# One key block of a query pair: split 256-column product against two 128-column products accumulated in PSUM

## The chip, the cores and the metric

One core of a Trainium2 chip runs the whole layer as a single program. The metric is the device time of one execution in microseconds; the median of several runs is compared.

## What is computed

The layer is a hybrid decoder layer: one input projection feeds eight stick-breaking attention heads, a short gated convolution, four memory cross-attention heads and a gate; the branch outputs are normalised by group, gated, projected back and added to the input. The change concerns only the stick-breaking attention (1024 tokens, 8 heads of 64):

```python
z = jnp.einsum('bqhd,bkhd->bhqk', q_blk, k, preferred_element_type=jnp.float32) * scale
before = key_pos[None, :] < q_pos[:, None]
log_not = jnp.where(before, jax.nn.log_sigmoid(-z), 0.0)
suffix = lax.cumsum(log_not, axis=3, reverse=True) - log_not
w = jnp.where(before, jnp.exp(jax.nn.log_sigmoid(z) + suffix), 0.0)
out = jnp.einsum('bhqk,bkhd->bqhd', w.astype(v.dtype), v)
```

All of it is float32.

## The kernel before

The sequence is held in reversed order, so the keys that a query may see lie at and behind its own position, and the stick-breaking products become forward scans along the keys. Float32 products run as several float32r products: each operand is split into hi (the value rounded to float32r) and lo (the exact rest).

Before the attention, the values of all heads are projected while the input arrives (`vh`, laid out as [key, head, hi and lo of 64 columns]). Then an attention part of 12 units runs: six stick-breaking heads, four memory heads, two stick-breaking heads. Each stick-breaking head (`sb_unit`) has four stages `sp` = 0 to 3. A stage takes a pair of query blocks of 128 tokens, blocks 2·sp and 2·sp + 1, against all key blocks from 2·sp on. `sb_scores` makes the scores (line 389, TensorE), the sigmoids (lines 396 and 397, ScalarE), the scan (lines 399 and 401, VectorE) and the weights (line 404, VectorE or GpSimd), for one query block at a time into an SBUF tile `sg`. `sb_apply_steps` then goes through the key blocks in groups `g` of two:

- `tr_step` transposes the weights' 128x128 blocks through TensorE (line 335) into one PSUM tile `tr`, in the order: second key block for both query blocks, first key block for both query blocks. In group 0 the first key block is the first query block's own: the second query block doesn't see it, and only three blocks are transposed.
- `transposed` then makes the hi `wth` by a ScalarE copy (line 341) and the lo `wtl` by a VectorE subtraction (line 342). Of a group's third and last block alone, the lo is written by a second subtraction (line 344) not into `wtl` but into `wth`, right behind the hi.
- `av_step` multiplies by the values: for each key block one product with the hi and one with the lo, 256 columns each (two query blocks), added up in the PSUM tile `av`, columns 0 to 255 (line 429). In group 0 the first key block is treated apart: one product of 256 columns, hi and lo of the one query block side by side (line 426), goes to columns 256 to 511 (`own`).

When the last group is done, `put_y` adds the upper and lower half of `av` (products with the hi and the lo of the values) into `y` by a ScalarE copy (line 351) and a VectorE addition (line 352). Then `put_own_key` does the same with `own` into a small tile (lines 358 and 359), and GpSimd adds its hi part and its lo part to the first query block's columns of `y` (line 361, twice). The small tile `avt` has one buffer; `av` has two, one PSUM bank each.

Between these steps the function `run` lays background work in proportion (`RATIO`, one number per unit): the other input projections (`proj`, line 273, the largest part of all products), the gates, the convolution and the memory's keys and values. Their input weights are split by lines 142 to 145. The instructions of each engine are put in order at build time by the framework's scheduler with a modelled timeline; each engine then works its list off in order, waiting on semaphores. `behind_attention` adds order-only dependencies that keep the projections from running ahead of the attention's transposes and scores.

After the attention come the output projection, the residual and the last norm (lines 760 to 819), which the change leaves alone.

Of the kernel before, what the change touches and what calls it, by code (L numbers as in the profile page):

```python
"""Hybrid decoder layer: stick-breaking attention, short gated convolution and memory
cross-attention heads side by side, group norms, SiLU gate, output projection.

The sequence is processed in reversed order (row j holds token T-1-j), so that the keys of a
query lie after it and the stick-breaking products are forward scans along the free axis:
  state[m] = max(state[m-1] * sigmoid(-z[m-1]), M[m]),   w[m] = sigmoid(z[m]) * state[m],
where M is one at the first key of the row and zero elsewhere.

Float32 products run as float32r passes: each operand is hi + lo, hi = the value rounded to
float32r, lo = the exact rest, and hi*hi + hi*lo + lo*hi carries float32's accuracy.  # L10
"""
# [15 lines left out]
P = 128  # L27
T = 1024
# [15 lines left out]
WARM = 8  # L44
# s, v, p: the engine (scalar, vector, pool) that rounds each weight tile, that takes each
# head's last product of the scan, and that splits its keys
WENG = 'vssssvvvsvvssvvsvvvssvvvvsss'
# [6 lines left out]
def hymba_kernel(ctx, tc, xT, xr, wp, wv, memT, memr, wmem, cols, eye, wout, gfin, out):  # L54
# [18 lines left out]
    def nm(s):  # L73
        uid[0] += 1
        return f"{s}_{uid[0]}"
# [20 lines left out]
    def f(ap):  # L96
        return ap.bitcast(F32)

# [1 line left out]
    col = const.tile([P, 32], F32, name="col")  # L100
# [46 lines left out]

# [1 line left out]
    def row_stats(j):  # L149
# [8 lines left out]

    # the tensor engine's clock comes up on work: zeros, while the first rows load
    for _ in range(WARM):  # L160
# [62 lines left out]

# [1 line left out]
    queue = []  # L225
# [16 lines left out]
    def behind_attention(ins):  # L242
        # order alone: keeps this work from running out ahead of the attention's steps
        if len(marks) > SLACK:
            tc.add_manual_dep(ins.ins, marks[-1 - SLACK].ins.name,
                              mybir.DependencyInfo(mybir.DependencyClass.NoSync, mybir.DependencyReason.DATA),
                              reason="pace")
# [3 lines left out]
    def proj_last(evac, need):  # L251
        # the input's tiles are done with one after the other: the output's weights take them
        wh, wl = next_w()
        ps = [z_tile(), z_tile()]
        for k in range(KC):
            for n, hf in enumerate(HALVES):
                for a, (ww, xx) in enumerate(((wh, xh), (wh, xl), (wl, xh))):
                    ins = nc.tensor.matmul(ps[n], lhsT=ww[:, k, :], rhs=xx[k][:, hf],
                                           start=(k == 0 and a == 0), stop=(k == KC - 1 and a == 2))
                    if a == 0:  # L260
                        behind_attention(ins)
            yield 1.3
        yield from after(need)
        for n, hf in enumerate(HALVES):
            evac(ps[n], hf)
# [65 lines left out]
    def transposed(blocks):  # L331
        # 4 [query, key] blocks: hi and lo of them; of a third and last one, lo comes after hi
        tr = tr_tile()
# [5 lines left out]
        n = len(blocks) * P  # L339
        m = n if n == H else 2 * P  # L340
        nc.scalar.copy(wh[:, 0:n], tr[:, 0:n])  # L341
        nc.vector.tensor_tensor(wl[:, 0:m], tr[:, 0:m], f(wh[:, 0:m]), op=ALU.subtract)  # L342
        if m < n:
            nc.vector.tensor_tensor(wh[:, n:], tr[:, m:n], f(wh[:, m:n]), op=ALU.subtract)
        return wh, wl
# [7 lines left out]

    def put_own_key(y, av, a, t0):
        # one block of queries times their own keys: w's hi, then its lo
        own, oth = (slice(0, 64), slice(64, 128)) if a == 0 else (slice(64, 128), slice(0, 64))
        tmp = small.tile([P, 256], F32, tag="avt", name=nm("avt"), bufs=1)
        nc.scalar.copy(tmp[own], av[oth])
        nc.vector.tensor_tensor(tmp[own], av[own], tmp[own], op=ALU.add)  # L359
        for c in (tmp[own, 0:P], tmp[own, P:]):  # L360
            nc.gpsimd.tensor_tensor(y[own, t0 : t0 + P], y[own, t0 : t0 + P], c, op=ALU.add)  # L361

    def interleave(first, second):
        # steps of two lists of (cost, function), in proportion
        ta, tb = sum(c for c, _ in first), sum(c for c, _ in second)
# [43 lines left out]
    def sb_apply_steps(st, sp, p, a):  # L409
# [9 lines left out]
        def av_step(g):  # L419
            if g == 0:  # L420
                st["av"] = av_tile(True)
            wh, wl = st.pop(("w", g))
            key = lambda j: vh[p][(2 * sp + 2 * g + j) // 4][:, (2 * sp + 2 * g + j) % 4, a, :]
            own, av = st["av"][:, 256:], st["av"][:, 0:256]
            if g == 0:
                nc.tensor.matmul(own, lhsT=key(0), rhs=wh[:, 256:], start=True, stop=True)
            for j, c in ((1, slice(0, 256)), (0, slice(256, H)))[: 2 if g else 1]:
                for n, w in enumerate((wh, wl)):
                    nc.tensor.matmul(av, lhsT=key(j), rhs=w[:, c], start=(g == 0 and n == 0),  # L429
                                     stop=(g == ng - 1 and j == (g == 0) and n == 1))  # L430
            if g == ng - 1:
                put_y(ys[p], av, a, 256 * sp)
                put_own_key(ys[p], own, a, 256 * sp)

# [19 lines left out]
    def stats_sum(st, g, first):  # L454
        # sums over the partitions, as a row, which a DMA lays out as [token, block]
        part = small.tile([P, TB], F32, tag="part", name=nm("part"), bufs=2)
# [13 lines left out]
    def group_stats(c):  # L470
        # the sums of squares of two tiles of 128 columns, a while later
        st = {}
# [99 lines left out]

# [1 line left out]
    def qk_proj(kinds, res):  # L574
# [119 lines left out]
    def attention(units):  # L694
        # steps of all heads in a row: the scores of a stage run one stage ahead of their use
        flat = []
# [15 lines left out]
    def run(steps, bg, ratio):  # L712
        # attention steps, with the other work in proportion
        debt = 0.0
# [44 lines left out]

# [1 line left out]
    post = ctx.enter_context(tc.tile_pool(name="post", bufs=2))  # L761
# [17 lines left out]
    for j in range(TB):  # L779
# [4 lines left out]
        for c in order:  # L784
# [4 lines left out]
                  (0, (0, 1, 2, 3), [tr_tile(), tr_tile()])]  # L789
        # the last rows end on half a bank: less is left to do after the last product  # L790
        todo = [(g, H * hf, H * hf + H) for g in range(3) for hf in range(2)]
# [77 lines left out]
```

## Time and profile before

| what | value |
| --- | --- |
| median of 3 runs | 613.98 us (613.79 to 614.02) |
| the profiled execution, from its first to its last instruction | 614.2 us |
| mean granted TensorE clock | 0.972 of full speed |
| matmuls / weight loads | 2744 / 2744 |
| VectorE, ScalarE, GpSimd instructions counted | 744, 775, 381 |

The profile is that of one execution; what lies around its span isn't recorded, and the span is 0.2 us above the runs' median. In the rows, PE is TensorE's matmuls, PEld its weight loads, DVE VectorE, ACT ScalarE, POOL GpSimd. A row of a group gives line, engine, operation, output and inputs by the program's names, shapes and count, then busy time in us and the mean of one in ns, then the idle time of the engine right before them and what ended it. A row of the timeline gives start and duration in us. A row of stretches gives its bounds and length, the busy time of the engines, the granted clock, the share of DMA and the GB/s.

### The profile page before, as it was taken

How to read it: one execution, taken by the hardware profiler on the slowest of the kernel's cores; microseconds unless marked ns; L12 is line 12 of the kernel's file. 1: busy time of each engine (PE TensorE's matmuls, PEld its weight loads, DVE VectorE, ACT ScalarE, POOL GpSimd, SP SyncE). 2: the span in 40 equal slices, each digit the busy share in tenths (PEclk: the TensorE clock that was granted, in tenths of full speed). 3: DMA queues.
4: the chain of work that ended last, by engine and by line, in shares of the span. 5: the costliest groups of instructions: out<-in, count | busy, mean ns of one | idle time of the engine just before them, and what ended most of it. 6: DMA issues, size and time to landing. Idle time of an engine off the chain costs nothing.

```text
span 614.2 us, 8410 instructions
## 1 busy us (share of the span) xinstructions
PE 565.8 (92%) x2744; PEld 461.6 (75%) x2744; DVE 454.3 (74%) x744; ACT 350.9 (57%) x775; POOL 338.7 (55%) x381
## 2 busy tenths in 40 slices
PE   9999989979899899877979999899988999899995
PEld 5888878758678688755768888778667886688884
DVE  3425159989999996579966766998779668977664
ACT  5646556536685777765745988563645554443232
POOL 2551787454247448987858657448789668411001
PEclk9999999979999999898979999899999999999998
DMA  8931520211302021121313212111011163131311
GB/s 283 403 107 36 137 67 16 57 36 35 104 34 67 5 68 35 34 56 70 98 53 104 70 35 69 34 36 35 4 32 35 35 240 103 69 138 68 114 59 69
DMA packets 22188, 48.36 MB, mean 79 GB/s; under 512 B 7808, under 2 KB 8320, under 8 KB 22144
## 3 DMA queue, kind: packets, MB, share of 16 engines
q1 hardware_dynamic: 22144, 47.82, 24.3%
q8 instruction: 22, 0.36, 0.2%
q14 instruction: 22, 0.18, 0.1%
HBM read 36.78 MB, written 4.20 MB: 67 GB/s over the span
## 4 chain that ended last, share of the span: by engine, by line
DVE 17%; PE 16%; ACT 7%; issue 7%; POOL 6%; DMA 2%; POOLq 0%; DVEq 0%; ACTq 0%
PE tr L802 6%; PE pj L273 3%; PE pj L802 3%; PE z L802 2%; DVE wtl L342 2%; ACT e L546 2%; DVE F L401 2%; DVE F L399 2%; POOL wlo L145 2%; DMA wor<-in_wout 1%; DVE whi L144 1%; POOL sg L404 1%; DVE wol L774 1%; DVE mx L542 1%; DVE y L352 1%
## 5 line engine op out<-in xcount | busy, mean ns | idle before, releaser
L273 PE MATMUL pj<-xh,whi 128*128 128x512 f32 x368 | 150.1, 408 | 4.1 <-DVE mv L681 3.4
L273 PE MATMUL pj<-xl,whi 128*128 128x512 f32 x368 | 146.5, 398 | 0.0
L273 PE MATMUL pj<-xh,wlo 128*128 128x512 f32 x368 | 146.1, 397 | 0.0
L145 POOL TENSOR_TENSOR wlo<-wraw,whi 128x512 fp32r<-128x512 f32 x56 | 81.5, 1469 | 16.2 <-ACT whi L142 11.0
L399 DVE TENSOR_TENSOR_SCAN F<-F,mask 128x513 f32<-128x513 f32 (+2 forms) x64 | 78.8, 1231 | 13.7 <-ACT F L396 11.0
L273 PEld LDWEIGHTS pj<-xh,whi 128*128 128x128 f32 x368 | 70.8, 192 | 17.2 <-DVE mv L681 3.6
L273 PEld LDWEIGHTS pj<-xh,wlo 128*128 128x128 f32 x368 | 70.5, 192 | 14.3
L273 PEld LDWEIGHTS pj<-xl,whi 128*128 128x128 f32 x368 | 70.7, 192 | 12.2
L396 ACT ACTIVATE F<-z,nrq 128x512 f32<-128x512 f32 (+3 forms) x96 | 55.8, 583 | 22.8 <-PE z L389 11.0
L404 POOL TENSOR_TENSOR sg<-sg,F 128x512 f32<-128x512 f32 (+3 forms) x48 | 56.0, 1171 | 20.1 <-DVE F L401 10.3
L342 DVE TENSOR_TENSOR wtl<-tr,wth 128x512 fp32r<-128x512 f32 (+1 forms) x96 | 56.1, 592 | 11.0 <-ACT wth L341 10.1
L361 POOL TENSOR_TENSOR y<-y,avt 64x128 f32<-64x128 f32 x64 | 47.5, 743 | 22.8 <-DVE avt L359 20.1
L341 ACT CAST wth<-tr 128x512 fp32r<-128x512 f32 (+1 forms) x96 | 51.1, 553 | 14.3 <-PE tr L335 12.7
L397 ACT ACTIVATE sg<-z,rq 128x512 f32<-128x512 f32 (+2 forms) x96 | 55.4, 580 | 3.0 <-PE tr L335 2.8
L335 PE MATMUL tr<-ident,sg 128*128 128x128 f32 x288 | 48.4, 285 | 5.6 <-DVE stg L462 2.0
L401 DVE TENSOR_TENSOR_SCAN F<-F,F,mask 128x512 f32<-128x512 f32 (+1 forms) x32 | 43.9, 1371 | 7.6 <-ACT F L396 7.0
L395 POOL MEMSET F<- 128x1 f32 x96 | 8.9, 97 | 72.0 <-DVE F L401 35.8
L814 POOL TENSOR_TENSOR ssf<-ssf,nhalf 128x1 f32<-128x1 f32 x8 | 7.4, 924 | 71.4 <-DVE ssf L811 62.1
L316 POOL TENSOR_TENSOR qs<-qk,q 64x512 fp32r<-64x512 f32 x24 | 32.9, 1377 | 23.9 <-ACT q L315 23.2
L335 PEld LDWEIGHTS tr<-ident,sg 128*128 128x128 f32 x288 | 35.7, 147 | 10.6 <-DVE sg L404 3.1
L429 PE MATMUL av<-wtl,vh 128*128 128x256 f32 x128 | 35.5, 295 | 7.6 <-DVE wtl L342 7.4
L389 PE MATMUL z<-k,q 128*128 128x512 f32 (+2 forms) x96 | 36.2, 377 | 3.1 <-ACT sg L397 2.9
(188 smaller groups left out, 1283.2 us busy)
## 6 DMA issues: line engine op xcount, KB each, us to landing
wraw<-in_wp SPq DMA_DIRECT2D x24, 512.0 KB, 3.3
xs<-in_xr SPq DMA_DIRECT2D x8, 512.0 KB, 8.6
wor<-in_wout SPq DMA_DIRECT2D x8, 512.0 KB, 5.3
acc<-in_xr SPq DMA_DIRECT2D x8, 512.0 KB, 3.4
out<-acc SPq DMA_DIRECT2D x16, 256.0 KB, 2.1
xs<-in_xT SPq DMA_DIRECT2D x7, 512.0 KB, 8.0
qs<-q SPq DMA_DIRECT2D x12, 256.0 KB, 2.9
q<-qs SPq DMA_DIRECT2D x12, 256.0 KB, 2.9
```

The costliest lines, as they stand in the source:

```text
L145: nc.gpsimd.tensor_tensor(lo[:, c], raw[:, c], f(hi[:, c]), op=ALU.subtract)
L273: ins = nc.tensor.matmul(ps, lhsT=ww[:, k, :], rhs=xx[k][:, hf], start=(k == 0 and a == 0), stop=(k == KC - 1 and a == 2))
L335: ins = nc.tensor.transpose(tr[:, i * P : (i + 1) * P], blk, ident)
L341: nc.scalar.copy(wh[:, 0:n], tr[:, 0:n])
L342: nc.vector.tensor_tensor(wl[:, 0:m], tr[:, 0:m], f(wh[:, 0:m]), op=ALU.subtract)
L361: nc.gpsimd.tensor_tensor(y[own, t0 : t0 + P], y[own, t0 : t0 + P], c, op=ALU.add)
L396: nc.scalar.activation(F[:, 1:m], zz[:, 0 : m - 1], AF.Sigmoid, scale=nrq[:, i : i + 1])
L397: nc.scalar.activation(sg[:, c0:c1], zz, AF.Sigmoid, scale=rq[:, i : i + 1])
L399: nc.vector.tensor_tensor_scan(F[:, 0:m], F[:, 0:m], M[:, 0:m], 0.0, ALU.mult, ALU.max)
L401: nc.vector.tensor_tensor_scan(F[:, 0:m], F[:, 0:m], M[:, 130 : 130 + m], prev[:, H - lo : H - lo + 1], ALU.mult, ALU.max)
L404: eng.tensor_tensor(sg[:, c0:c1], sg[:, c0:c1], F[:, 0:w], op=ALU.mult)
L802: nc.tensor.matmul(ps[:, pc], lhsT=yy[:, c, :], rhs=ww[c][:, c0:c1], start=(c == cs[0] and a == 0), stop=(c == cs[-1] and a == 2))
```

## The change

The first key block of group 0 is no longer treated apart. Its hi lies in `wth` and its lo in `wtl` like that of every other block (one subtraction of 384 columns in place of 256 and 128), and it is multiplied by two products of 128 columns, hi and lo, that accumulate in the first 128 columns of `av`. Line 426's product, `put_own_key` and the second half of `av` go; key block 1 comes first and starts the accumulation.

```diff
 def transposed(blocks):
     ...
     n = len(blocks) * P
-    m = n if n == H else 2 * P
     nc.scalar.copy(wh[:, 0:n], tr[:, 0:n])
-    nc.vector.tensor_tensor(wl[:, 0:m], tr[:, 0:m], f(wh[:, 0:m]), op=ALU.subtract)
-    if m < n:
-        nc.vector.tensor_tensor(wh[:, n:], tr[:, m:n], f(wh[:, m:n]), op=ALU.subtract)
+    nc.vector.tensor_tensor(wl[:, 0:n], tr[:, 0:n], f(wh[:, 0:n]), op=ALU.subtract)
     return wh, wl
 ...
-def put_own_key(y, av, a, t0):
-    own, oth = (slice(0, 64), slice(64, 128)) if a == 0 else (slice(64, 128), slice(0, 64))
-    tmp = small.tile([P, 256], F32, tag="avt", name=nm("avt"), bufs=1)
-    nc.scalar.copy(tmp[own], av[oth])
-    nc.vector.tensor_tensor(tmp[own], av[own], tmp[own], op=ALU.add)
-    for c in (tmp[own, 0:P], tmp[own, P:]):
-        nc.gpsimd.tensor_tensor(y[own, t0 : t0 + P], y[own, t0 : t0 + P], c, op=ALU.add)
 ...
     def av_step(g):
         if g == 0:
-            st["av"] = av_tile(True)
+            st["av"] = av_tile()
         wh, wl = st.pop(("w", g))
         key = lambda j: vh[p][(2 * sp + 2 * g + j) // 4][:, (2 * sp + 2 * g + j) % 4, a, :]
-        own, av = st["av"][:, 256:], st["av"][:, 0:256]
-        if g == 0:
-            nc.tensor.matmul(own, lhsT=key(0), rhs=wh[:, 256:], start=True, stop=True)
-        for j, c in ((1, slice(0, 256)), (0, slice(256, H)))[: 2 if g else 1]:
+        av = st["av"]
+        for j, c in ((1, slice(0, 256)), (0, slice(256, H if g else 256 + P))):
             for n, w in enumerate((wh, wl)):
-                nc.tensor.matmul(av, lhsT=key(j), rhs=w[:, c], start=(g == 0 and n == 0),
-                                 stop=(g == ng - 1 and j == (g == 0) and n == 1))
+                nc.tensor.matmul(av[:, 0 : c.stop - c.start], lhsT=key(j), rhs=w[:, c],
+                                 start=(g == 0 and j == 1 and n == 0),
+                                 stop=(g == ng - 1 and j == 0 and n == 1))
         if g == ng - 1:
             put_y(ys[p], av, a, 256 * sp)
-            put_own_key(ys[p], own, a, 256 * sp)
```

The remaining lines of the diff only blank out comments.

## The prediction

> **What bounds the kernel now.** I read the page's busy table first, then the stretches, then single starts in the timeline.
>
> ```profile
> span 614.2 us, 8410 instructions
> PE 565.8 (92%) x2744; PEld 461.6 (75%) x2744; DVE 454.3 (74%) x744; ACT 350.9 (57%) x775; POOL 338.7 (55%) x381
> ```
>
> TensorE is busy for most of the span, but ends of matmuls are modelled there, so the share says only that it comes first. The attention lies between about 85 and 505 us. In the table by stretch (length, then busy time and count of PE, PEld, DVE, ACT, POOL, then the granted clock) its three parts are the first stick-breaking heads, the memory heads, and the last two stick-breaking heads:
>
> ```profile
> 85.00:310.00 225.00, 197.03 (x1032) 164.29 (x1030) 197.72 (x282) 144.59 (x302) 141.40 (x192) 0.95 0.18 51
> 310.00:395.00 85.00, 82.53 (x416) 68.65 (x417) 60.03 (x121) 60.28 (x140) 53.54 (x53) 0.96 0.24 64
> 395.00:505.00 110.00, 102.80 (x510) 83.19 (x509) 88.00 (x131) 57.09 (x124) 76.49 (x82) 0.98 0.17 58
> ```
>
> From 85 to 310 us TensorE and VectorE are both busy for 197 of 225 us: they hold each other up in turn. After that TensorE alone is near full. So work added to TensorE counts wherever it doesn't fall into one of its waits, and work taken from VectorE counts only where TensorE waits for it.
>
> What one product really costs TensorE is the distance from its start to the next start, not its row's duration. The timeline has all the widths close together:
>
> ```profile
> 171.62 0.33 PE L389 MATMUL z<-k,q 128*128 128x384 f32 x1
> 171.79 0.34 PE L389 MATMUL z<-k,qs 128*128 128x384 f32 x1
> ...
> 174.03 0.39 PE L273 MATMUL pj<-xl,whi 128*128 128x512 f32 x1
> 174.26 0.39 PE L273 MATMUL pj<-xh,wlo 128*128 128x512 f32 x1
> 174.48 0.28 PE L389 MATMUL z<-k,q 128*128 128x256 f32 x1
> 174.60 0.28 PE L389 MATMUL z<-k,qs 128*128 128x256 f32 x1
> 174.72 0.60 PE L335 MATMUL tr<-ident,sg 128*128 128x128 f32 x4
> 175.07 0.48 PE L273 MATMUL pj<-xh,whi 128*128 128x512 f32 x1
> 175.40 0.40 PE L273 MATMUL pj<-xl,whi 128*128 128x512 f32 x1
> ```
>
> 512 columns take 0.23 us (174.03 to 174.26), 384 take 0.17 (171.62 to 171.79), 256 take 0.12 (174.48 to 174.60): a straight line of 0.45 ns a column. The four 128-column transposes and the 512-column product behind them take 175.40 − 174.72 = 0.68 us, so a transpose costs (0.68 − 0.23)/4 = 0.11 us, twice what that line gives for 128 columns (0.06).
>
> **The change, part by part.** It touches a place that occurs 32 times: 8 heads by 4 pairs of query blocks, the first pair of key blocks of each (g = 0).
>
> ```profile
> L426 PE MATMUL av<-wth,vh 128*128 128x256 f32 x32 | 10.9, 340 | 12.9 <-DVE wth L344 10.8 <-ACT sg L397 1.2 <-ACT avt L351 0.9
> L429 PEld LDWEIGHTS av<-wth,vh 128*128 128x128 f32 x128 | 24.5, 192 | 3.1 <-ACT wth L341 0.2 <-issue 0.2 <-ACT avt L358 0.2
> L342 DVE TENSOR_TENSOR wtl<-tr,wth 128x512 fp32r<-128x512 f32 x64 | 43.2, 682 | 8.7 <-ACT wth L341 8.2
> L342 DVE TENSOR_TENSOR wtl<-tr,wth 128x256 fp32r<-128x256 f32 x32 | 13.2, 413 | 2.2 <-ACT wth L341 1.9
> L344 DVE TENSOR_TENSOR wth<-tr,wth 128x128 fp32r<-128x128 f32 x32 | 8.9, 279 | 0.0
> L359 DVE TENSOR_TENSOR avt<-av,avt 64x256 f32<-64x256 f32 x32 | 13.3, 414 | 3.3 <-ACT avt L358 2.9
> L358 ACT COPY avt<-av 64x256 f32<-64x256 f32 x32 | 11.7, 366 | 20.6 <-DVE y L352 20.2
> L361 POOL TENSOR_TENSOR y<-y,avt 64x128 f32<-64x128 f32 x64 | 47.5, 743 | 22.8 <-DVE avt L359 20.1
> ```
>
> *TensorE.* One 256-column product (line 426, hi and lo side by side) goes, two 128-column products with the same key come: 768 columns before and after, one matmul and one weight load more. The weight load is hidden: 192 ns rows run beside products that start every 0.12 us. The price of a 128-column float32r product is the open number, since no row has one. Below, the straight line gives 0.06 us: then nothing is added. The nearest row by width, the transpose, gives 0.11: 2 × 0.11 − 0.12 = +0.10 a place. Above, it should not cost more than the 512-column product, 0.23: +0.34 a place, 10.9 us over 32. I take 0.23. This is a choice, not a reading: the transpose already stands at twice the line, so the line doesn't hold at 128 columns, and a transpose, which passes one operand through unchanged, is to me a floor for a product of that width; 0.23 is the only row above it that bounds one.
>
> The Trainium skill, "FP8 and Floating Point Precision", section TensorE Precision Notes, states that true float32 takes four passes through the array. If a narrow float32r product fell back to that, 4 × 128 columns would cost what the 512 row costs, and the total would be the 617.4 worked out below; with one pass it would be 606.5. No row before the change can tell which.
>
> *The wait at line 426.* The own-key product needs the lo that line 344 writes, behind line 342's first subtraction. The first and the last place of those that wait:
>
> ```profile
> 90.83 0.28 DVE L344 TENSOR_TENSOR wth<-tr,wth 128x128 fp32r<-128x128 f32 x1
> 91.26 0.36 PE L426 MATMUL av<-wth,vh 128*128 128x256 f32 x1 [1.06 <-DVE wth L344]
> ...
> 475.99 0.28 DVE L344 TENSOR_TENSOR wth<-tr,wth 128x128 fp32r<-128x128 f32 x1
> 476.42 0.36 PE L426 MATMUL av<-wth,vh 128*128 128x256 f32 x1 [1.46 <-DVE wth L344]
> ```
>
> In 14 of the 32 places, these two the outermost, line 426 starts within 0.15 us of line 344's end; in the other 18 the lo has long been there. Afterwards the first product (key 1, hi) needs only ScalarE's copy, so it slips into the wait (0.12 us), and the wait moves to the second product, which needs one subtraction of 384 columns. That lies between the 256 and 512 rows, (0.413 + 0.682)/2 = 0.55 us, against 0.413 + 0.279 = 0.69: the lo is ready 0.15 us sooner. Queued behind it on TensorE's in-order stream are that place's last three products, then transposes and scores. So a waiting place costs 0.34 − 0.12 − 0.15 = +0.07 us, an unhindered one +0.34: 14 × 0.07 + 18 × 0.34 = **+7.1 us**.
>
> *VectorE.* Line 359 goes (0.414) and the split subtraction saves 0.15: 0.56 us a place, 18 us of 454. It counts where VectorE is what TensorE waits for. At most that is all 14 waiting places, 7.8 us; at least nothing. I take half, **−3.9 us**: line 359 comes after the last product of its pair, and what the next wait needs may be held by a scan or a copy instead.
>
> *ScalarE and GpSimd.* The copies at line 358 (11.7 us) and the adds at line 361 (47.5 us) go. Nothing of TensorE's reads y soon; the waits they end are these:
>
> ```profile
> PE av L426 <- DVE wth L344: 10.8, 10, 2.1
> ACT avt L351 <- POOL y L361: 15.3, 9, 4.2
> ACT avt L358 <- DVE y L352: 20.2, 17, 3.8
> ```
>
> The second and third (engine, what it waited for, us in total, times, longest) hold ScalarE, which is idle 43% of the span; I count them as nothing of their own. If that cover is gone, they are worth up to what ScalarE then delivers late, and that is inside the 7.8 us above. The PSUM tile is free one copy and one add sooner; with two such tiles nobody is shown waiting for it. No DMA and no queue entry of SyncE moves.
>
> **Sum.** 614.2 + 7.1 − 3.9 = 617.4 us on the profiled execution's span; that span is 0.2 above the median of the runs, 613.98, so 617.2 for the median. The three runs lie within 0.04%; I take 0.2%, 1.2 us, as what can be told from no change.
>
> **The rivals.**
>
> *Narrow products are cheap (faster).* At 0.11 us: 18 × 0.10 + 14 × (0.10 − 0.27) − 3.9 = −4.5, 609.7 us; at 0.06: 14 × (−0.27) − 3.9 = −7.7, 606.5. For it speaks the nearest row by width, against it that this row is no product. It decides as soon as the price is under about 0.18 us: 32 × (2 × 0.18 − 0.12) = 7.7 is what the 14 places (14 × 0.27 = 3.8) and the relief (3.9) give back.
>
> *Narrow products are dear, but GpSimd's adds were in VectorE's way (faster).* A scan beside a GpSimd multiply takes far longer than its kind does in the mean:
>
> ```profile
> 91.66 1.29 POOL L404 TENSOR_TENSOR sg<-sg,F 128x512 f32<-128x512 f32 x1
> 91.73 1.77 DVE L401 TENSOR_TENSOR_SCAN F<-F,F,mask 128x256 f32<-128x256 f32 x1
> ...
> L399 DVE TENSOR_TENSOR_SCAN F<-F,mask 128x256 f32<-128x256 f32 x8 | 6.7, 832 | 0.1
> ```
>
> 1.77 against 0.83 us for 256 columns. If a quarter of the removed 47.5 us had stood in VectorE's way, that is 11.9 us, of which 14/32 counts: 5.2; with the whole of VectorE's 7.8 the sum is 614.2 + 7.1 − 13.0 = 608.3. It decides when the relief passes 7.1 us, 0.22 a place. Against it: the adds are of 64 partitions by 128 columns, mostly short, and they come when a pair is finished.
>
> The Trainium skill, "SBUF — State Buffer", section Who interferes with whom, has a VectorE instruction with two SBUF inputs shut out while a GpSimd instruction reads SBUF; the slow scan agrees. By that rule all 47.5 us could block, which would double this rival's gain.
>
> *The terms cancel (no change).* With the whole 7.8 us of relief and no more, the sum is 613.5.
>
> *The order shifts (slower still).* Instructions are put in order by a modelled timeline, which the changed products shift. What an unlucky order costs shows in two neighbouring stretches:
>
> ```profile
> 120.00:140.00 20.00, 15.77 (x73) 12.93 (x73) 17.04 (x26) 8.61 (x19) 8.20 (x14) 0.83 0.08 27
> 140.00:160.00 20.00, 19.91 (x109) 16.79 (x108) 19.17 (x30) 12.29 (x25) 7.10 (x10) 1.00 0.36 105
> ```
>
> TensorE loses 4.2 us in the first and 0.1 in the second, and the clock falls to 0.83 beside the loss. One more such stretch gives 617.4 + 4.1 = 621.5; with no relief either, 614.2 + 10.9 = 625.
>
> **How the numbers follow.** Dear products with half the relief (617.4): 0.50. A worse order on top (621 to 625): 0.10. Cancelling: 0.15. GpSimd's relief: 0.10. Cheap products: 0.15. So faster 0.25, same 0.15, slower 0.60. The range 607 to 625 reaches from nearly the cheap end, 606.5, to no relief at all, 625; for the likeliest case alone it is 613.5 to 625, slower than no change nearly throughout.
>
> **What would show it.** Right: 64 products of 128 columns in the attention at about 0.23 us from start to start where they don't wait; the wait for line 344 gone and a shorter one for line 342 in the same 10 to 14 places; VectorE down by some 18 us and GpSimd by some 47; TensorE's busy time up by 7 to 11. Wrong: starts 0.06 to 0.12 us apart behind the narrow products; scans markedly shorter on VectorE; or the same stage taking another order with other waits.

## The result: 22 us faster, and the profile after

The changed kernel takes 591.57 us (median of 4 runs, 590.72 to 592.65), the kernel before 613.88 beside it: ratio 0.9644, interval 0.9609 to 0.9680. The forecast was 617.2, range 607 to 625.

Page of the changed kernel, its span and busy times:

```profile
span 590.1 us, 8309 instructions
...
PE 556.6 (94%) x2776; PEld 460.2 (78%) x2776; DVE 426.6 (72%) x680; ACT 340.0 (58%) x743; POOL 300.5 (51%) x317
```

VectorE has 27.7 us less (18 were forecast; for the other 9.8 its remaining instructions got shorter), GpSimd 38.2 less (the additions were 47.5; what is left on it lasts longer), and TensorE, with 32 products more, is busy 9 us *less*. The table by stretch shows where:

```profile
85.00:310.00 225.00, 208.76 (x1148) 176.90 (x1147) 193.33 (x264) 147.31 (x307) 129.32 (x162) 0.98 0.20 58
310.00:395.00 85.00, 81.13 (x413) 67.66 (x412) 66.80 (x118) 61.46 (x138) 46.70 (x46) 0.98 0.20 54
395.00:505.00 110.00, 104.54 (x514) 85.55 (x514) 79.68 (x113) 53.87 (x115) 75.37 (x67) 0.99 0.23 76
```

From 85 to 310 us TensorE gets through 1148 products where it got through 1032; 24 of the 116 more are the added ones. The gain is TensorE waiting less, and a granted clock of 0.98 in place of 0.95, not less work for it.

The changed place itself, by groups (the last number is idle time ahead and what ended it):

```profile
L341 DVE TENSOR_TENSOR wtl<-tr,wth 128x384 fp32r<-128x384 f32 x32 | 17.5, 547 | 5.1 <-ACT wth L340 4.8
...
L416 PE MATMUL av<-wtl,vh 128*128 128x128 f32 x32 | 8.9, 279 | 0.0
L416 PE MATMUL av<-wth,vh 128*128 128x128 f32 x32 | 7.2, 226 | 0.0
```

and one such place in the timeline (start, duration):

```profile
185.55 0.28 PE L416 MATMUL av<-wtl,vh 128*128 128x256 f32 x1
185.67 0.22 PE L416 MATMUL av<-wth,vh 128*128 128x128 f32 x1
185.73 0.28 PE L416 MATMUL av<-wtl,vh 128*128 128x128 f32 x1
185.85 0.51 PE L335 MATMUL tr<-ident,sg 128*128 128x128 f32 x3
```

with the weight loads of the same stretch:

```profile
185.55 0.19 PEld L416 LDWEIGHTS av<-wth,vh 128*128 128x128 f32 x1
185.68 0.19 PEld L416 LDWEIGHTS av<-wtl,vh 128*128 128x128 f32 x1
185.81 0.31 PEld L335 LDWEIGHTS tr<-ident,sg 128*128 128x128 f32 x3
```

The first narrow product gives way after 0.06 us, in 30 of the 32 places (in the other two, at half the granted clock, after 0.11). The second gives way after 0.11 to 0.12 in 31 of 32, whatever follows it. Its successor's load starts 0.13 us after its own, and I read it so that the load sets the pace: in the kernel before, no two loads of line 429's products start less than 0.108 us apart at full clock. That is some 0.17 for both narrow products, where the removed product took 0.12: +0.05 us a place, 1.6 us in all, where +0.34 at an unhindered place was forecast. The narrow products never wait (idle 0.0); the wait for VectorE's one subtraction now comes at the 256-column product with the lo. From the list of waits (us in total, times, longest), of the changed kernel:

```profile
PE av L416 <- DVE wtl L341: 13.5, 10, 3.8
```

and of the kernel before, where this stands beside line 426's 10.8:

```profile
PE av L429 <- DVE wtl L342: 7.4, 5, 3.7
```

Together 18.2 us in 15 waits became 13.5 in 10.

### The profile page after: what moved, and what is told of

It is laid out like the page before. It is cut to its first block, busy times and chain, and to the rows that moved or that the text cites. A ratio compares the mean times of both kernels' runs of the same rounds, so it can differ in the third digit from the quotient of the medians.

```text
span 590.1 us, 8309 instructions
## 1 busy us (share of the span) xinstructions
PE 556.6 (94%) x2776; PEld 460.2 (78%) x2776; DVE 426.6 (72%) x680; ACT 340.0 (58%) x743; POOL 300.5 (51%) x317
## 4 chain that ended last, share of the span: by engine, by line
PE 32%; DVE 12%; issue 5%; ACT 3%; POOL 2%; DMA 2%; SPq 1%; POOLq 0%; DVEq 0%; ACTq 0%
PE pj L273 11%; PE tr L789 7%; PE pj L789 4%; PE z L789 3%; DVE wtl L341 2%; DVE F L389 2%; PE z L258 2%; DVE F L387 2%; PE tr L335 2%; PE av L416 1%; DMA part<-stg 1%; POOL sg L392 1%; PE z L527 1%; DVE whi L144 1%; DVE sg L392 1%
## 5 line engine op out<-in xcount | busy, mean ns | idle before, releaser
L273 PE MATMUL pj<-xh,whi 128*128 128x512 f32 x368 | 147.2, 400 | 1.0 <-DVE mv L668 1.0
L273 PEld LDWEIGHTS pj<-xh,whi 128*128 128x128 f32 x368 | 69.4, 189 | 12.7 <-DVE mv L668 1.2
L392 POOL TENSOR_TENSOR sg<-sg,F 128x512 f32<-128x512 f32 (+3 forms) x48 | 62.2, 1298 | 27.6 <-DVE F L389 10.5
L341 DVE TENSOR_TENSOR wtl<-tr,wth 128x512 fp32r<-128x512 f32 (+1 forms) x96 | 59.7, 637 | 9.9 <-ACT wth L340 9.1
L416 PE MATMUL av<-wtl,vh 128*128 128x256 f32 (+1 forms) x160 | 43.3, 303 | 13.6 <-DVE wtl L341 13.5
L389 DVE TENSOR_TENSOR_SCAN F<-F,F,mask 128x512 f32<-128x512 f32 (+1 forms) x32 | 41.7, 1304 | 8.7 <-ACT F L384 6.4
L416 PEld LDWEIGHTS av<-wtl,vh 128*128 128x128 f32 x160 | 31.3, 196 | 20.3 <-DVE wtl L341 18.0
L416 PE MATMUL av<-wth,vh 128*128 128x256 f32 (+1 forms) x160 | 45.1, 287 | 0.0
L335 PEld LDWEIGHTS tr<-ident,sg 128*128 128x128 f32 x288 | 34.2, 144 | 9.2 <-POOL sg L392 3.9
```

Of the source, the lines that this page charges most:

```text
L273: ins = nc.tensor.matmul(ps, lhsT=ww[:, k, :], rhs=xx[k][:, hf], start=(k == 0 and a == 0), stop=(k == KC - 1 and a == 2))
L335: ins = nc.tensor.transpose(tr[:, i * P : (i + 1) * P], blk, ident)
L341: nc.vector.tensor_tensor(wl[:, 0:n], tr[:, 0:n], f(wh[:, 0:n]), op=ALU.subtract)
L389: nc.vector.tensor_tensor_scan(F[:, 0:m], F[:, 0:m], M[:, 130 : 130 + m], prev[:, H - lo : H - lo + 1], ALU.mult, ALU.max)
L392: eng.tensor_tensor(sg[:, c0:c1], sg[:, c0:c1], F[:, 0:w], op=ALU.mult)
L416: nc.tensor.matmul(av[:, 0 : c.stop - c.start], lhsT=key(j), rhs=w[:, c], start=(g == 0 and j == 1 and n == 0), stop=(g == ng - 1 and j == ...
```

## The experiments

All but the last two of these kernels hold each engine's instructions in the order that the kernel before has, or the changed one where that is said, by order-only dependencies, so that the planner's choice doesn't mix into the comparison:

```diff
+        seq = [mine[n] for n in np.frombuffer(zlib.decompress(base64.b85decode(packed)), np.int16)]
+        for one, nxt in zip(seq, seq[1:]):
+            tc.add_manual_dep(nxt, one.name, ..., reason="order")
```

Ratios are to the kernel before on the same chip, with 95% intervals; 0.001 is 0.61 us.

**Is it the order?** The changed work in before's order, and before's work in the changed kernel's order; in both nothing but the order-only dependencies above is added.

> The changed kernel, with every engine's instructions held in the order that the kernel before has (order-only dependencies; the two narrow products stand right behind their place's second product). Theory work (what was removed from VectorE, ScalarE and GpSimd and from the wait at the own-key product shortens TensorE's waits, whatever the order): about 592 us, as the changed kernel. Theory order (the planner happened on a better order, and the work itself is nearly neutral, since the narrow products cost 0.06 and 0.11 us): 608 to 614 us.

> The kernel before, with every engine's instructions held in the order that the changed kernel has; the own-key product stands right ahead of its place's first product, and the copies, additions and the split subtraction that the changed kernel lacks are put in by the planner. Theory work: about 614 us, as the kernel before. Theory order: 592 to 600 us.

Measured: 0.9648 (0.9610 to 0.9686) and 1.0280 (1.0233 to 1.0327). In before's order the change gains as much as in its own. The second lies outside both expectations: the new order, with the instructions that it lacks put in by the planner, costs before's work 17 us. So the gain is in the work.

**Which half of the work?** The new products and the single subtraction with `put_own_key` left running (on the first half of `av`, so that `y` is another one), and the old products with `put_own_key` left out.

```diff
 # products only: as the change, but at the end of av_step
+                put_own_key(ys[p], av, a, 256 * sp)
 # without put_own_key: as before, but
-                put_own_key(ys[p], own, a, 256 * sp)
```

> In the order of the kernel before: the changed products and the single subtraction of 384 columns, but the copy, the addition and GpSimd's two additions of put_own_key are kept (they read av's first half and add it to y once more, so y is another one). Theory work in the form that VectorE's and GpSimd's removed work counts most: 606 to 612 us. Theory that the moved wait counts (the own-key product no longer stands first and waits for the second subtraction): 592 to 600 us. Theory order: 608 to 614.

> In the order of the kernel before: the kernel before with put_own_key left out (its copy, addition and GpSimd's two additions; the own-key block is multiplied but never added to y). Theory work by VectorE and GpSimd: 592 to 600 us. Theory of the moved wait: 608 to 614 us, as the wait at the own-key product stays. Theory order: 608 to 614.

Measured: 0.9990 (0.9969 to 1.0010) and 0.9657 (0.9632 to 0.9682). The products and the subtraction are worth nothing either way, −0.6 us (−1.9 to +0.6). From the waits of the kernel with the products alone:

```profile
PE av L425 <- DVE wtl L341: 15.3, 13, 3.8
```

18.2 us of waiting became 15.3, which pays for the 1.6 us that the narrow products cost. All of the gain that can be told from noise comes from leaving `put_own_key` out.

**Which part of `put_own_key`?** Only GpSimd's additions left out; only ScalarE's copy and VectorE's addition left out; the additions moved to VectorE.

```diff
 # no additions on GpSimd
-            nc.gpsimd.tensor_tensor(y[own, t0 : t0 + P], y[own, t0 : t0 + P], c, op=ALU.add)
 # additions only
-        nc.scalar.copy(tmp[own], av[oth])
-        nc.vector.tensor_tensor(tmp[own], av[own], tmp[own], op=ALU.add)
-        for c in (tmp[own, 0:P], tmp[own, P:]):
+        for c in (ident[own, :], ident[own, :]):
 # additions on VectorE
-            nc.gpsimd.tensor_tensor(...)
+            nc.vector.tensor_tensor(...)
```

> In the order of the kernel before: GpSimd's two additions of line 361 left out, the copy at line 358 and the addition at line 359 kept (the own-key block is never added to y). Theory GpSimd (the 47 us of additions make its multiplies of the weights and what follows late): about 592 us. Theory buffer (ScalarE, in order, stands before its copies into the one-buffer tile avt until GpSimd has read it, 15.3 us, and until VectorE has, 20.2 us, and the sigmoids and hi copies behind stand with it): the larger part of the gain, 595 to 602 us, as the second wait stays. Theory VectorE (line 359 and the shared time): 608 to 614 us.

> In the order of the kernel before: the copy and the addition of lines 358 and 359 left out, GpSimd's two additions kept, but reading a constant tile of the same shape in place of avt (y is another one). Theory GpSimd: 608 to 614 us. Theory buffer: about 592 us, since nothing but put_y uses avt. Theory VectorE: 596 to 604 us, VectorE's 13 us being gone and GpSimd's additions still in its way.

> In the order of the kernel before, all of its work, but the two additions of line 361 on VectorE, right behind line 359. Theory queue: GpSimd is free of 47 us, and VectorE gets 64 additions of about 0.25 us, some 16 us more: 600 to 608 us. Theory reading: the same range or less, 597 to 606, as VectorE's own additions hold nobody up. Theory that the own-key additions cost wherever they stand: 612 to 618 us.

Measured: 0.9721 (0.9690 to 0.9751), 0.9907 (0.9876 to 0.9938) and 1.0035 (1.0009 to 1.0061). Without the additions 17.1 us go (15.3 to 19.0), and the copy with VectorE's addition makes about 4 more (0.9721 against 0.9657). The first time lies where the theory of the held buffer had it; the kernel with the constant, below, shows that this proves nothing for that theory. On VectorE the same additions take 39.9 us and cost 2 us more than on GpSimd, though GpSimd's queue and the reading beside it are then free: the work has no free place on either engine.

```profile
L361 DVE TENSOR_TENSOR y<-y,avt 64x128 f32<-64x128 f32 x64 | 39.9, 623 | 2.2
```

**How do GpSimd's additions reach TensorE?** One place shows the first way, in the timeline of the kernel before:

```profile
123.58 2.05 POOL L361 TENSOR_TENSOR y<-y,avt 64x128 f32<-64x128 f32 x2 [0.24 <-DVE avt L359]
...
125.63 2.50 POOL L145 TENSOR_TENSOR wlo<-wraw,whi 128x512 fp32r<-128x512 f32 x2
125.67 0.37 ACT L351 COPY avt<-av 64x256 f32<-64x256 f32 x1 [3.27 <-POOL F L395]
126.06 0.69 ACT L396 ACTIVATE F<-z,nrq 128x512 f32<-128x512 f32 x1
...
126.85 3.59 DVE L399 TENSOR_TENSOR_SCAN F<-F,mask 128x513 f32<-128x513 f32 x1 [0.36 <-ACT F L396]
...
127.38 0.44 PE L389 MATMUL z<-k,q 128*128 128x384 f32 x1 [1.10 <-ACT sg L397]
```

and of the kernel without the additions, in the same order:

```profile
123.61 0.37 ACT L351 COPY avt<-av 64x256 f32<-64x256 f32 x1 [1.19 <-DVE avt L359]
124.00 0.69 ACT L394 ACTIVATE F<-z,nrq 128x512 f32<-128x512 f32 x1
...
124.59 3.50 POOL L145 TENSOR_TENSOR wlo<-wraw,whi 128x512 fp32r<-128x512 f32 x2
...
125.64 1.39 DVE L397 TENSOR_TENSOR_SCAN F<-F,mask 128x513 f32<-128x513 f32 x1
...
126.34 0.33 PE L387 MATMUL z<-k,q 128*128 128x384 f32 x1
...
127.13 1.51 DVE L402 TENSOR_TENSOR sg<-sg,F 128x512 f32<-128x512 f32 x1
```

The additions hold the one buffer of `avt` until 125.6 (the memset named as releaser stands right behind them). ScalarE's next copy into it waits 3.27 us, and behind that copy, in ScalarE's list, stand the sigmoids that free TensorE's `z` and feed the scan. "Nothing of TensorE's reads y soon" was true; what is late next is the buffer that the additions *read*. The next kernels take this apart: the additions read a constant in place of `avt`, so nothing is held; they keep one column of 128; in place of each, seven one-column memsets that read nothing (with the rest of `put_own_key` out).

```diff
 # constant
-        for c in (tmp[own, 0:P], tmp[own, P:]):
+        for c in (ident[own, :], ident[own, :]):
 # one column
-        for c in (tmp[own, 0:P], tmp[own, P:]):
+        for c in (tmp[own, 0:1], tmp[own, P : P + 1]):
-            nc.gpsimd.tensor_tensor(y[own, t0 : t0 + P], y[own, t0 : t0 + P], c, op=ALU.add)
+            nc.gpsimd.tensor_tensor(y[own, t0 : t0 + 1], y[own, t0 : t0 + 1], c, op=ALU.add)
 # memsets
+        for _ in range(14):
+            nc.gpsimd.memset(warm[:, 0:1], 0.0)
```

> In the order of the kernel before, all of its work kept, but GpSimd's two additions of line 361 read a constant tile of the same shape in place of avt (y is another one): they no longer hold the one buffer and no longer wait for line 359. Theory GpSimd: 612 to 615 us. Theory buffer: 598 to 604 us. Theory VectorE: 612 to 615 us.

> In the order of the kernel before, all instructions kept, but GpSimd's two additions of line 361 take one column of 128 each (y lacks the rest of the own-key block): the waits and the hold on avt are as before, only the additions' length goes. Theory GpSimd (its time counts): 592 to 598 us. Theory buffer (the place in the chain counts, copy, addition, GpSimd in turn): 604 to 612 us. Theory VectorE: 608 to 614 us.

> In the order of the kernel before: put_own_key's copy and addition left out, and each of GpSimd's additions replaced by seven memsets of one column (98 ns each in the profiles, 0.69 us together, as long as an addition there), which read nothing from SBUF (the own-key block is never added to y). Theory queue (what costs is that GpSimd is busy and its next instructions start later): 606 to 611 us, as with the additions alone. Theory reading (the additions' reads hold up VectorE's scans and multiplies, whose second operand also comes from SBUF): 592 to 597 us, as without put_own_key.

Measured: 0.9973 (0.9952 to 0.9995), 0.9824 (0.9795 to 0.9853) and 0.9841 (0.9798 to 0.9884). The last two times lie between the ranges of their theories. So the held buffer is not the main thing: without it 1.7 us go. The same place in the timeline of the kernel with the constant shows why so little:

```profile
123.10 3.78 POOL L361 TENSOR_TENSOR y<-y,ident 64x128 f32<-64x128 f32 x2
123.39 0.37 ACT L351 COPY avt<-av 64x256 f32<-64x256 f32 x1 [1.20 <-DVE avt L359]
123.78 0.69 ACT L396 ACTIVATE F<-z,nrq 128x512 f32<-128x512 f32 x1
...
126.74 4.40 DVE L404 TENSOR_TENSOR sg<-sg,F 128x512 f32<-128x512 f32 x1
126.88 2.48 POOL L145 TENSOR_TENSOR wlo<-wraw,whi 128x512 fp32r<-128x512 f32 x2
```

The sigmoid is 2.3 us earlier (126.06 to 123.78), but the two additions last 3.78 us in place of 2.05, and VectorE's multiply beside GpSimd's splits of line 145 takes 4.40 us. Without the additions those splits start 2.3 us earlier (124.59, not 126.88) and are nearly done when the multiply starts; it takes 1.51. So the additions also act by pushing what stands behind them in GpSimd's list onto VectorE's work. The 2 us won at ScalarE are lost at VectorE. Yet shared reading isn't all either: 47.4 us of memsets, which read nothing, cost 11 us of the gain (0.9841 against 0.9657),

```profile
L358 POOL MEMSET warm<- 128x1 f32 x448 | 47.4, 106 | 23.4
...
L398 DVE TENSOR_TENSOR_SCAN F<-F,F,mask 128x256 f32<-128x256 f32 x16 | 16.8, 1048 | 4.4 <-POOL warm L358 4.2
```

here by what stands behind them in GpSimd's list: scans, among others, start late behind "warm" (4.2 us of it in this row). The pages of the kernels without the copy and VectorE's addition show the reading apart from the queue; without additions, with memsets for them, and with additions of the constant:

```profile
PE 552.5 (94%) x2744; PEld 454.6 (77%) x2744; DVE 435.2 (74%) x712; ACT 339.0 (57%) x743; POOL 297.0 (50%) x317
```

```profile
PE 554.7 (93%) x2744; PEld 454.9 (76%) x2744; DVE 431.4 (72%) x712; ACT 339.0 (57%) x743; POOL 339.4 (57%) x765
```

```profile
PE 559.4 (92%) x2744; PEld 458.5 (76%) x2744; DVE 447.4 (74%) x712; ACT 338.5 (56%) x743; POOL 336.4 (55%) x381
```

VectorE runs the same 712 instructions in all three. The memsets don't make them longer (431.4 against 435.2 us), so their 11 us come by the queue, with VectorE's work no longer than before; the additions, which read, make it 12 us longer (447.4). In run time the additions cost 4 us more than the memsets (0.9907 against 0.9841), but these two intervals overlap a little, so how much of the 17 us is reading is not settled. The one-column additions still take 27.3 us (below) and give 11 of the 17 us.

Two more ask *what* in GpSimd's list is delayed: in the kernel before, the memsets of `F`, which stand right behind most additions, moved to VectorE; and, in the kernel with the constant, the additions moved later in GpSimd's list (its only edit besides is the order).

```diff
-            nc.gpsimd.memset(F[:, 0:1], 0.0 if prev is None else 1.0)
+            nc.vector.memset(F[:, 0:1], 0.0 if prev is None else 1.0)
```

> The kernel before, whole, in its own order, with one thing moved: the 96 memsets of column 0 of F (line 395) are issued by VectorE right before their scan, no longer by GpSimd, where in most places they stand behind the additions of line 361. Theory A (the additions delay mainly these memsets, and with them sigmoids and scans): most of the 17 us that leaving out the additions gave comes back, 598 to 604 us. Theory B (the delay is carried by the other instructions in GpSimd's list, the multiplies of line 404 and the splits of line 145, by the one-buffer tile avt and by shared reading): no more than a per cent, 608 to 616 us; VectorE has 96 short instructions more.

> The kernel of the additions that read the constant (613.4 us), with nothing but the place of the additions in GpSimd's list changed: 53 of the 64 stand 1 to 8 instructions later, 34 of them behind the next two memsets of line 395, as far as no reader of y comes in between. They still add a constant in place of avt. Theory A (their place in GpSimd's queue is the cost): the work behind them starts sooner and the time falls by 5 to 10 us, to 603 to 608 us. Theory B (GpSimd's total time and its reading beside VectorE is the cost, wherever it stands): within 0.5%, 610 to 616 us.

Measured: 1.0099 (1.0074 to 1.0124) and 1.0046 (1.0023 to 1.0069). Theory A fell both times, and both kernels are slower than theory B's range too: 96 short memsets moved to VectorE cost 6 us in all, additions later in the list 4.5 (against 0.9973). The second speaks against the additions' place as what carries the cost. The first doesn't rule out the memsets, as what their earlier start won and what VectorE lost by them can't be told apart. I read it so: in this stage neither VectorE nor GpSimd has slack, and what is added to either comes out somewhere. Which instruction of GpSimd's list hands the delay on was not isolated.

**Why does it cost so much?** The row of granted clock on the pages (40 slices, in tenths), first of the kernel before, then of the changed one, then of that without `put_own_key`:

```profile
PEclk9999999979999999898979999899999999999998
```

```profile
PEclk9999999999999999989899999889999999999999
```

```profile
PEclk9999999999999999999999999899999999999998
```

The dips are stretches of 3.41 us, or twice that, at exactly half. In the kernel before there are seven between 85 and 505 us; four of them by stretch (the clock is the third number from the end):

```profile
128.70:135.53 6.83, 4.41 (x14) 3.75 (x15) 6.62 (x11) 3.12 (x7) 2.68 (x5) 0.50 0.24 79
166.30:169.71 3.41, 3.14 (x10) 2.76 (x11) 3.35 (x5) 1.43 (x3) 0.20 (x2) 0.50 0.00 0
248.20:251.61 3.41, 3.41 (x13) 3.01 (x12) 2.60 (x4) 3.41 (x8) 3.15 (x7) 0.50 0.00 0
...
395.00:398.41 3.41, 3.41 (x14) 2.83 (x13) 3.27 (x5) 1.02 (x3) 0.10 (x1) 0.50 0.00 0
```

They are not idle time: TensorE is busy there, at half speed. In the timeline of the kernel before, behind one wait:

```profile
166.57 1.33 PE L335 MATMUL tr<-ident,sg 128*128 128x128 f32 x5 [1.66 <-DVE sg L404]
...
168.55 0.63 PE L273 MATMUL pj<-xh,wlo 128*128 128x512 f32 x1
168.97 0.63 PE L273 MATMUL pj<-xh,whi 128*128 128x512 f32 x1
```

512 columns take 0.42 us, not 0.23. The Trainium skill, "TensorE: Matmul & The Clock Gate", section Part 1: The HAM clock gate, has this: a free-running window of about 3.4 us, and half rate after an idle one. The stretches agree in length and rate. But the windows need not be idle throughout. I summed what the products of each window of 3.41 us take at full clock (0.06, 0.12, 0.17 and 0.23 us for the four widths), between 85 and 505 us of 17 profiles of this case. 81 windows at full clock were followed by one at half, and in them TensorE streamed 0 to 0.40 of the time; of the 1892 that were not, the emptiest streamed 0.34, and only 32 no more than 0.40. So the edge lies at a bit over a third: 2.0 to 2.3 us without streaming in one window are enough.

That can make a wait dear. Taking for each product in such a stretch the distance to the next start above that of its width at full clock, and no more than the same again, the seven stretches cost 11.6 us in the kernel before, four in the changed kernel 5.4, one in the kernel without `put_own_key` 1.4. Of the 24.1 us between the spans of before and after, 6.2 are of this kind, and of the 24.1 to the kernel without `put_own_key` 10.2. Whether that is a cost of its own was tried by adding work: products that compute nothing, meant to lie in waits ahead of four of before's seven stretches and ahead of all four of the changed kernel's (in its own order). They are called ahead of a transposition or of `av_step`'s first product; the order list puts each at its place.

```diff
+    warm = lambda kind, t: [nc.tensor.matmul(t, lhsT=M[:, 0:P], rhs=M[:, 0 : t.shape[1]], start=True, stop=True) for _ in range(warm_count(kind))]
```

> The kernel before, whole and in its own order, with 42 products added that compute nothing (512 columns of a constant, 12 of them 256 columns; about 8 us of TensorE work), each set ahead of a wait of TensorE that the profile of before has just in front of a stretch at a granted clock of 0.50: 8 ahead of two waits for z at 127.4 and 129.0, 8 ahead of line 426 at 131.9, 12 ahead of the transposes at 166.6, 7 ahead of line 426 at 247.9, 7 ahead of line 562 at 393.5. Theory C (a wait costs twice: the idle time, and then a half-speed clock for 3.4 us or a multiple; this second part makes up about half of what the change gained): the added work lies in the waits, the four stretches at 0.50 that it aims at (128.7 to 135.5, 166.3, 248.2 and 395.0) stay at full clock, and the time falls by 3 to 6 us, to 608 to 611 us. Rival (the half clock only goes with the waits and costs nothing beside them, or the added products come in the way): no change or slower, 614 to 620 us.

> The changed kernel in its own order with 34 such products of 512 columns added ahead of its four waits in front of a half-speed stretch: 12 ahead of line 416 at 261.4, 8 ahead of line 653 at 285.4, 7 ahead of line 549 at 372.8, 7 ahead of line 416 at 394.2. Theory C: up to 5.4 us (four stretches, 1.2 to 1.5 us each), 586 to 589 us. Rival: 591 to 596 us.

Measured: 0.9967 (0.9949 to 0.9985) and 0.9645 (0.9618 to 0.9671). With 42 useless products the kernel before is 2 us *faster*, and in its profile the four stretches are at full clock:

```profile
128.70:135.53 6.83, 6.13 (x32) 4.18 (x31) 6.62 (x11) 3.05 (x7) 2.73 (x5) 1.00 0.24 79
166.30:169.71 3.41, 3.27 (x19) 2.60 (x18) 3.35 (x7) 2.47 (x7) 0.56 (x2) 1.00 0.00 0
248.20:251.61 3.41, 3.41 (x20) 2.92 (x19) 2.60 (x4) 3.19 (x7) 3.33 (x4) 1.00 0.00 0
395.00:398.41 3.41, 3.41 (x17) 2.89 (x16) 3.37 (x7) 3.35 (x8) 0.00 (x0) 1.00 0.00 0
```

The work that stood in the last two rows runs some 5 us earlier here; it ran at full clock too, as no stretch at half lies between 85 and 275 us or between 290 and 505. The seven added products of the last place ran behind their wait of 1.84 us, not in it. So the half clock is a cost of its own, but less than I expected of it (3 to 6 us), and less than my count: the three stretches whose waits were filled are 4.7 us by it, and the time fell by 2.0 (0.9 to 3.1). Either the count is too high or the added work took part of it back. The 12 runs of the filled kernel have mean clocks of 0.979 to 0.992, the 17 of before beside them 0.969 to 0.983. The kernel filled after the change is no test of it. Three of its four fills ran behind the wait that they were meant for. In its list of waits the added products (line 224) themselves waited:

```profile
PE tr L224 <- DVE wtl L341: 7.8, 3, 3.8
```

They write into `tr`, and the releaser is VectorE's subtraction, whose input is such a tile. At two of these waits, of 3.76 and 2.20 us, the clock is at half again.

**Versions of the changed kernel.** Memsets of `F` on VectorE, and the multiplies of two of the four heads that GpSimd has on VectorE, both in an order of the planner's choice.

```diff
-            nc.gpsimd.memset(F[:, 0:1], 0.0 if prev is None else 1.0)
+            nc.vector.memset(F[:, 0:1], 0.0 if prev is None else 1.0)
 # the other
-MENG = 'pvvvppvp'
+MENG = 'pvvvvvvp'
```

> The changed kernel with the one-column memsets of F on VectorE in place of GpSimd (96 of 0.1 us), order left to the planner. Theory queue: ScalarE's sigmoids no longer stand behind GpSimd's long subtractions and multiplies, 584 to 591 us. Theory reading: nothing gained, 591 to 595 us, as VectorE gets 96 instructions more.

> The changed kernel with the last multiplies of the heads 4 and 5 on VectorE in place of GpSimd, order left to the planner. Theory queue and theory reading both: GpSimd loses some 32 us of multiplies, VectorE gets half as much and no reads against it, 584 to 592 us; if VectorE is now the tighter of the two, 593 to 600 us.

Measured: 0.9670 (0.9617 to 0.9723) and 0.9633 (0.9591 to 0.9675), the changed kernel's 0.9644 within both. No version beats it, though the second has 27.2 us less on GpSimd and 9.6 more on VectorE.

## Why the prediction was wrong, step by step

| term | forecast, us | what the runs showed, us |
| --- | --- | --- |
| products and the wait at line 426 | +7.1 | −0.6 (−1.9 to +0.6), the subtraction in it |
| VectorE's relief | −3.9 | about −4, with ScalarE's copy |
| ScalarE and GpSimd | 0 | −17.1 (GpSimd's additions alone) |
| sum | +3.2 | −21.7; measured −21.9 |

*The products.* "I take 0.23 … a transpose … is to me a floor for a product of that width" failed. The transposes' 0.11 was no floor: a narrow product costs 0.06, what the straight line gave, and the second 0.11 to 0.12. "The weight load is hidden" failed too, by my reading: two narrow products in a row go at the pace of their loads, and the transposes' 0.11 is the distance of their loads as well (median 0.109). The Trainium skill, "TensorE: Matmul & The Clock Gate", section Wait — 56ns, not 53.3ns?, gives 55.6 ns from start to start for 128 columns at full clock; its example is bf16. The 0.06 agrees, and the fallback to four passes that I weighed didn't occur. The line had three points, the row against it was another operation. By the low rival's price (0.06 to 0.11) this term would have been −3.8 to −0.6; the measured one is at the upper end of that.

*The wait.* Right: it goes to the one subtraction (0.547 us, 0.55 was estimated), and the products alone shorten the waiting by 2.9 us, where 14 × (0.12 + 0.15) = 3.8 was in the sum. With 1.6 us for the products in place of 32 × 0.34, the step's own working gives 1.6 − 3.8 = −2.2, with the measured 2.9 it gives −1.3; measured are −0.6 (−1.9 to +0.6).

*VectorE.* Half of 7.8 was about right in size, in part by luck: the half was a choice, ScalarE's copy is in what was measured, and the split subtraction is not. It is read off twice, each time to some 2.4 us either way: the copy and VectorE's addition left out make 3.9 us where GpSimd's additions are gone (0.9721 to 0.9657) and 4.1 where they are kept (0.9973 to 0.9907).

*ScalarE and GpSimd.* This step decided. "I count them as nothing of their own … inside the 7.8 us above" failed: the term put at nothing measured 17.1 us. The cover was taken from an average: GpSimd at 55% and ScalarE idle 43% of the span hide that, from 85 to 310 us, VectorE is busy for 198 of 225 us and GpSimd for 141, and each holds up the other by reading, by order in the queue and by the buffer. The row that pointed at it, 15.3 us of ScalarE waiting for these additions, was quoted and put aside because ScalarE is idle elsewhere, though sigmoids stand behind the waiting copy. It pointed at the place, not at the price: the additions that read a constant end these waits, and that was worth 1.7 us.

*The rivals.* "GpSimd's adds were in VectorE's way" named the mechanism nearest to what happened, and asked for a quarter of the 47.5 us times 14/32, 5.2 us; it was 17.1. The row against it ("mostly short, and they come when a pair is finished") was no measure of what waits behind them. The row for it was read against the wrong kind: the scan of 1.77 us has three inputs, and its own kind has a mean of 1.17, not 0.83:

```profile
L401 DVE TENSOR_TENSOR_SCAN F<-F,F,mask 128x256 f32<-128x256 f32 x16 | 18.7, 1171 | 1.1 <-ACT F L396 0.7
```

That the whole 47.5 us "would double this rival's gain" was a wrong sum. Times 14/32 they are 20.8, and the rival's own working then gives 614.2 + 7.1 − 7.8 − 20.8 = 592.7 us, beside a measured span of 590.1. That nearness is luck: the +7.1 in it was wrong, and 11 us also came of memsets that read nothing. The Trainium skill, "SBUF — State Buffer", section Who interferes with whom, has the rule for GpSimd instructions that read SBUF, not for those that only write it. The multiply at 4.40 us beside GpSimd's reading agrees, and so do VectorE's 712 instructions, longer beside the additions and not beside the memsets. "Narrow products are cheap" was right in its price and would have missed 15 us.

*The clock.* I quoted a stretch at 0.83 and gave it to an unlucky order. It was a term: with 11.6 us lost to half speed by my count, the waits that went count more than their length. By that count, which is rather an upper bound, the 24.1 us of the changed kernel are 17.9 of other loss and 6.2 of half clock, and the 24.1 without `put_own_key` are 13.9 and 10.2.

## What to carry to other kernels

Two engines that are each busy for most of a stage, and hold each other up by a list, a buffer or reads of the same memory, may have no idle time to hide small work in: price a removed instruction there at its whole duration as the other bound, not at nothing (here 17 of 47.5 us came back). Follow a wait on a side engine to what stands behind the waiting instruction in its list. And look for stretches at half clock behind TensorE's waits: a wait of some 2 us can cost more than its length. How much more is open here; filling three such waits brought 2 us.

## What the runs showed of the hardware that I had not expected

- A 128-column float32r product starts its successor after 0.06 us, or 0.11 to 0.12 behind another such product, where I take the next weight load to set the pace; a 128-column transpose takes 0.11.
- In 17 profiles TensorE's clock halved for 3.41 us or a multiple behind every window of that length with less than 0.34 of streaming, behind none with more than 0.40, and behind some between; idle throughout the window need not be.
- A GpSimd addition of 64 partitions by one column takes 426 ns in the mean, of 128 columns 743; at the least 183 and 448. Some two fifths to over half of it doesn't depend on the size.

```profile
L361 POOL TENSOR_TENSOR y<-y,avt 64x1 f32<-64x1 f32 x64 | 27.3, 426 | 22.8 <-DVE avt L359 20.2
```

- Open: how much of the 17 us is GpSimd's reading and how much its queue, what the half clock costs in the changed kernel, and whether 0.34 to 0.40 is one sharp edge that my sum blurs.
